# Strassen's seven block products for most of the down projection, in a one-core float32 decoder trunk

## The chip, the cores and the metric

The kernel runs on one core of a Trainium2 chip. The metric is the device time of one execution in microseconds (us), the median of three runs. The engines are named as the profile names them: PE (matmul) with PEld (its weight load), DVE (VectorE), ACT (ScalarE), POOL (GpSimd) and SP (SyncE, whose queue issues most loads).

## The reference, cut to what matters

One layer over 512 tokens of width 1024: a SwiGLU, a token mixer, a second SwiGLU, each added to the running `x`. The change touches the two SwiGLUs only.

```
D_MODEL, SEQ, D_FF, DEPTH = 1024, 512, 2816, 1
def swiglu(x, w_gate, w_up, w_down):
    return (jax.nn.silu(x @ w_gate) * (x @ w_up)) @ w_down
...
x = x + 0.5 * swiglu(rms_norm(x, ffn1_norm[i]), ffn1_w_gate[i], ffn1_w_up[i], ffn1_w_down[i])
x = x + token_mixer(rms_norm(x, mix_norm[i]), ...)
x = x + 0.5 * swiglu(rms_norm(x, ffn2_norm[i]), ffn2_w_gate[i], ffn2_w_up[i], ffn2_w_down[i])
```

## The kernel before, in words

Every float32 product in question is made of three matmuls: an operand is split into a high part of type float32r and a low part (the rest), and high times high, high times low and low times high are summed in PSUM (`mm3`, L443; the matmul itself is L448). A split of weights is one ACT copy (`whi`, L100) and one subtraction (`wlo`, L101); a split of activations is the same pair in `split` (L453, L454).

The hidden width 2816 is cut into 22 tiles of 128 columns, called ff tiles here. `ffn` (L505) goes through them in eleven rounds p, two ff tiles a round. A round makes the gate tiles g0 and g1 (24 matmuls of 512 tokens each), then the up tiles u0 and u1. After a gate tile ACT takes a tanh of it (`th`, L517) and DVE makes `m` (L519). After an up tile DVE makes the activation `a` (L524), and `a` is split into `ah` and `al`. Gate tiles go to the three PSUM banks of `mm`, up tiles and down products to the three of `sc`.

The down projection is laid between the gate and the up tiles. In rounds 2, 4, 6 and 8 `down` (L556) multiplies a chunk of four finished ff tiles by their rows of the down weights: 2 column halves x 4 token tiles x 4 ff tiles x 3 = 96 matmuls of 512 columns. Each of its eight PSUM tiles is added to the running `x` on DVE by one instruction (`add_x`, L541). Round 9 does ff tiles 16 and 17, and after the last round comes a tail with ff tiles 18 to 21, both through `down_tile` (L543).

`Weights` (L61) streams all weights in one fixed order. `load` (L77) issues a DMA of 1 MB on SP's queue into one of two raw buffers; `split` (L85) splits the next part; `get` (L107) asks for a part that is to be used now; `bg` (L114) splits one more part if it is at most two (by default) ahead of the one in use. The split parts lie in four buffers each of `whi` and `wlo`. In the SwiGLUs the subtraction is on DVE (`self.sub`). Each engine does its instructions in the order in which the program gives them, and a waiting instruction holds what is behind it.

The pool `big2` has six tiles of 128x2048, four of which hold the normalised input `hT` in a SwiGLU. The pool `big` has 19 tiles of 128x1024 (`t4`) for `x`, the split activations and much else. After round 0 the hook `hook0` (L634) issues six small loads on POOL's queue (`setup_loads`, L395), and after round 2 `hook2` (L637) does small work with them (`setup_work`, L413), two small matmuls on PE among it.

Of the kernel before, what the change touches and what calls it, by code (L numbers as in the profile page):

```python
# [11 lines left out]
F32 = mybir.dt.float32  # L12
# [48 lines left out]
class Weights:  # L61


    def __init__(self, nc, raw_pool, pool, specs, ahead_load):
        self.nc, self.raw_pool, self.pool, self.specs = nc, raw_pool, pool, specs
# [6 lines left out]
        self.order = [(s, p) for s, spec in enumerate(specs) for p in range(len(spec[1]))]  # L72
# [12 lines left out]
    def split(self, last):  # L85
        nc = self.nc
        while self.n_split <= min(last, len(self.order) - 1):
            i = self.n_split
            s, p = self.order[i]
            self.load(s)  # L90
            src = self.specs[s][1][p](self.raws[s])
            a, b = src.shape[1], src.shape[2]
            if (self.specs[s][2], p) in self.held:
# [7 lines left out]
            self.sub.tensor_tensor(l, src, h.bitcast(F32), op=ALU.subtract)  # L101
            self.parts[s, p] = (h, l)
            self.n_split += 1
            if p == len(self.specs[s][1]) - 1:
                self.load(s + self.ahead_load)

    def get(self, name, p):  # L107
        s = self.ids[name]
        i = self.first[s, p]
        self.split(i)  # L110
        self.cur = max(self.cur, i)
        return self.parts[s, p]
# [87 lines left out]
def hybrid_trunk_kernel(ctx: ExitStack, tc: tile.TileContext, x, rel_bias, ffn1_norm, ffn1_w_gate, ffn1_w_up,  # L200
# [42 lines left out]
    specs = []  # L243

    def cols(w, name, c0):

        def view(raw):
            return raw.rearrange("p (k c) -> p k c", k=8)
        specs.append(([(view, w[:, c0:c0 + 256].rearrange("(k p) c -> p k c", p=128))],
                      [lambda raw, g=g: view(raw)[:, :, g * 128:g * 128 + 128] for g in range(2)], name))  # L250

    def cols256(w, name, c0):
# [4 lines left out]
        specs.append((loads, parts, name))  # L257

    def rows(w, name, r0, nk, c0, nc_):
# [5 lines left out]
        specs.append((loads, parts, name))  # L265
# [19 lines left out]
    for i in range(2):  # L285
        src = w_in[512 * i:512 * i + 512]
        specs.append(([(lambda raw, o=o, n=n: c_view(raw)[:, :, o:o + n],
                        src[:, c:c + n].rearrange("(k p) c -> p k c", p=128))
                       for o, c, n in ((0, C_Q, 384), (384, IDX_K, 72))],
                      [lambda raw, h=h: c_view(raw)[:, 2 * h:2 * h + 2, :] for h in range(2)], f"c{i}"))  # L290
# [3 lines left out]
    def cols2x(name, c0, c1):  # L294
# [5 lines left out]
        specs.append((loads, [lambda raw, h=h: view(raw)[:, 4 * h:4 * h + 4, :] for h in range(2)], name))  # L300
# [9 lines left out]
    def row_cols(w, name):  # L310

        def view(raw):
            return raw.rearrange("p (k c) -> p k c", k=2)
        specs.append(([(view, w.rearrange("(k p) c -> p k c", p=128))],
                      [lambda raw, h=h: view(raw)[:, :, 512 * h:512 * h + 512] for h in range(2)], name))
# [21 lines left out]
    W = Weights(nc, rawp, wsp, specs, 2)  # L337
# [167 lines left out]
    def ffn(f, hT, order, hooks, after_tile):  # L505
# [25 lines left out]
        def down_terms(c, nk, t, wparts, csl):  # L531
            terms = []
            per = nk // 2
            for k in range(nk):
                w = wparts[k // per]
                ah, al = aT[4 * c + k]
                terms.append((ah[:, tok(t)], al[:, tok(t)], w[0][:, k % per, csl], w[1][:, k % per, csl]))
            return terms

        def add_x(ps, t, csl):  # L540
# [825 lines left out]
```

## Time and profile before

| | |
|---|---|
| median of three runs | 1312.66 us (1312.38 to 2589.32) |
| the profiled execution | 1312.75 us |
| its span, first to last instruction | 1310.8 us |
| mean granted TensorE clock | 0.997 of full speed |

The span is what the views of the trace cover. The profiled execution has 1.95 us outside of it. One of the three runs, 2589.32 us, is about twice as long as the other two and is left out of the comparison.

### The profile page before, as it was taken

To read this page: it belongs to the slowest core of one execution; us is meant where nothing else is said; L and a number is where in the kernel's file an instruction comes from. 1 tells how busy PE (TensorE), PEld (TensorE's weight loads), DVE (VectorE), ACT (ScalarE), POOL (GpSimd) and SP (SyncE) were. 2 spreads that over 40 slices of the span, in tenths; PEclk is the share of its full clock that TensorE was granted. 3 is DMA by queue.
4 is the path that set the end of the run, shared out by engine and by line. 5 is a ranking of instruction groups with operands and counts; after the bars stand their busy time and mean duration, and the time that the engine had idled before them with its cause. 6 is when DMAs were issued, how large, how long until landed. Compare 5 with 4: busy or idle time off the path is not lost.

```text
span 1310.8 us, 17140 instructions
## 1 busy us (share of the span) xinstructions
PE 1293.1 (99%) x6976; PEld 1097.5 (84%) x6976; DVE 677.9 (52%) x1265; ACT 451.7 (34%) x832; POOL 153.7 (12%) x137
## 2 busy tenths in 40 slices
PE   9999999999999999999989999999999999999998
PEld 8887888888889889889877778888898888888887
DVE  4444444445464666587854564447644444444453
ACT  4322222222343545454566432233332222222220
POOL 3000000000011435446340000000000000000000
PEclk9999999999999999999999999999999999999999
DMA  6233323222332222222222034423232323332321
GB/s 202 97 97 116 96 96 96 97 97 96 122 129 68 95 82 77 86 65 81 65 82 62 23 102 137 157 68 106 87 97 96 97 96 97 96 97 96 96 96 65
DMA packets 101777, 125.07 MB, mean 95 GB/s; under 512 B 3817, under 2 KB 85225, under 8 KB 101698
## 3 DMA queue, kind: packets, MB, share of 16 engines
q1 hardware_dynamic: 96690, 114.08, 27.1%
q10 hardware_dynamic: 3456, 5.24, 1.2%
q0 software_dynamic: 1552, 4.65, 1.2%
q8 instruction: 55, 0.90, 0.3%
q14 instruction: 24, 0.20, 0.0%
HBM read 119.13 MB, written 4.84 MB: 95 GB/s over the span
## 4 chain that ended last, share of the span: by engine, by line
PE 92%; DVE 3%; ACT 2%; DMA 1%; issue 0%; POOL 0%; ACTq 0%; DVEq 0%
PE u L448 18%; PE dn L448 18%; PE g L448 18%; PE gt L448 10%; PE wo L448 3%; PE br L448 3%; PE iq L448 2%; PE c L448 2%; PE b0q L448 1%; PE a0q L448 1%; PE a0v L448 1%; PE a0k L448 1%; PE a2q L448 1%; PE a1v L448 1%; PE b0v L448 1%; PE a1k L448 1%
## 5 line engine op out<-in xcount | busy, mean ns | idle before, releaser
L100 ACT ACTIVATE whi<-raw 128x1024 fp32r<-128x1024 f32 (+1 forms) x210 | 218.8, 1051 | 182.3 <-PE dn L448 141.2
L101 DVE TENSOR_TENSOR wlo<-raw,whi 128x1024 fp32r<-128x1024 f32 (+1 forms) x178 | 216.3, 1220 | 75.4 <-ACT whi L100 75.1
L448 PE MATMUL dn<-whi,ah 128*128 128x512 f32 x352 | 137.1, 389 | 0.0
L448 PE MATMUL dn<-whi,al 128*128 128x512 f32 x352 | 137.0, 389 | 0.0
L448 PE MATMUL dn<-wlo,ah 128*128 128x512 f32 x352 | 136.9, 389 | 0.0
L541 DVE SCALAR_TENSOR_TENSOR x<-dn,x 128x512 f32<-128x512 f32 x96 | 65.8, 690 | 108.3 <-PE dn L448 108.1
L453 ACT ACTIVATE ah<-a 128x512 fp32r<-128x512 f32 x44 | 27.8, 632 | 190.2 <-DVE a L524 190.2
L519 DVE SCALAR_TENSOR_TENSOR m<-th,g 128x512 f32<-128x512 f32 x44 | 30.2, 687 | 116.2 <-ACT th L517 116.2
L101 POOL TENSOR_TENSOR wlo<-raw,whi 128x1024 fp32r<-128x1024 f32 x32 | 76.7, 2397 | 28.6 <-ACT whi L100 18.6
L524 DVE TENSOR_TENSOR a<-m,u 128x512 f32<-128x512 f32 x44 | 30.2, 687 | 95.4 <-PE u L448 95.4
L448 PEld LDWEIGHTS dn<-whi,al 128*128 128x128 f32 x352 | 66.1, 188 | 13.8
L448 PEld LDWEIGHTS dn<-wlo,ah 128*128 128x128 f32 x352 | 66.1, 188 | 13.7
L448 PEld LDWEIGHTS dn<-whi,ah 128*128 128x128 f32 x352 | 66.1, 188 | 13.6
L448 PE MATMUL gt<-rmh,wlo 128*128 128x512 f32 x192 | 76.2, 397 | 0.0
L448 PE MATMUL gt<-rml,whi 128*128 128x512 f32 x192 | 76.0, 396 | 0.0
L448 PE MATMUL gt<-rmh,whi 128*128 128x512 f32 x192 | 76.0, 396 | 0.0
L517 ACT ACTIVATE th<-g 128x512 f32<-128x512 f32 x44 | 26.3, 597 | 139.3 <-PE g L448 139.3
L448 PE MATMUL g<-hal,whi 128*128 128x512 f32 (+1 forms) x192 | 71.4, 372 | 0.3 <-DVE hal L454 0.3
L448 PE MATMUL g<-hah,whi 128*128 128x512 f32 (+1 forms) x192 | 71.6, 373 | 0.1
L448 PE MATMUL g<-hah,wlo 128*128 128x512 f32 (+1 forms) x192 | 71.4, 372 | 0.2 <-POOL wlo L101 0.2
L448 PE MATMUL g<-hbh,whi 128*128 128x512 f32 (+1 forms) x192 | 71.4, 372 | 0.0
L448 PE MATMUL u<-hah,wlo 128*128 128x512 f32 (+1 forms) x192 | 71.4, 372 | 0.0
(1086 smaller groups left out, 3042.8 us busy)
## 6 DMA issues: line engine op xcount, KB each, us to landing
raw<-in_w_in SPq DMA_DIRECT2D x25, 1024.0 KB, 5.1
raw<-in_ffn_w_gate SPq DMA_DIRECT2D x22, 1024.0 KB, 5.2
raw<-in_ffn_w_up SPq DMA_DIRECT2D x22, 1024.0 KB, 5.1
raw<-in_ffn_w_down SPq DMA_DIRECT2D x22, 1024.0 KB, 4.9
raw<-in_w_in SPq DMA_DIRECT2D x8, 512.0 KB, 4.5
raw<-in_w_out SPq DMA_DIRECT2D x4, 1024.0 KB, 4.7
x<-in_x SPq DMA_DIRECT2D x4, 512.0 KB, 6.5
x1d<-x ACTq DMA_DIRECT2D x4, 512.0 KB, 2.7
```

Source lines behind the costliest of these rows:

```text
L100: nc.scalar.activation(h, src, AF.Copy)
L101: self.sub.tensor_tensor(l, src, h.bitcast(F32), op=ALU.subtract)
L448: nc.tensor.matmul(ps, l, r, start=i == 0 and q == 0, stop=i == n - 1 and q == 2)
L453: nc.scalar.activation(hi, src, AF.Copy)
L517: nc.scalar.activation(th, g, AF.Tanh, scale=0.5)
L519: nc.vector.scalar_tensor_tensor(m, th, 1.0, g, op0=ALU.add, op1=ALU.mult)
L524: nc.vector.tensor_tensor(a, m, u, op=ALU.mult)
L541: nc.vector.scalar_tensor_tensor(xt[t][:, csl], ps, 0.25, xt[t][:, csl], op0=ALU.mult, op1=ALU.add)
```

## The change

The first sixteen ff tiles (four chunks c of four) are multiplied by Strassen's scheme. For a pair of ff tiles the left operand is cut into four blocks: even or odd ff tile, first or second 256 tokens. The weights of a chunk are cut likewise: even or odd rows of 128, left or right half of the 1024 columns. Seven products replace eight. A product has two PSUM tiles of 128 tokens by 512 columns, and each of them takes 2 pairs x 3 = 6 matmuls of 512 columns, 12 for the product.

- **Left sums.** `left_blocks` makes five sums or differences of 128x256 for a pair of ff tiles on POOL. Splits of 128x256, 128x1024 and 128x512 for each pair follow on ACT and DVE, the last two of them (`split_sums`) only after the next gate or up tile has been issued.
- **Weight sums.** A new class `Blocks` loads a chunk's 2 MB as two tiles into the two free tiles of `big2` and makes five sums of 128x1024 for a chunk on POOL, most of them in place. The split of each of the seven weight blocks has its subtraction on POOL and no longer on DVE. The loads of the next chunk are issued on SP when the seventh block of this one is split, and have to wait until that split has been done.
- **Results.** Two products out of three go into two blocks of the output: a chunk has 24 additions to `x` in place of 8.
- **Order.** In rounds 2 to 9 one product (`down_block`) comes after each gate or up tile: four in an even round, three in an odd one. Their PSUM tiles alternate between `mm` and `sc`. The split order is written out as `plan`.
- **Moved.** Ff tiles 16 and 17 are multiplied in round 10 and not in round 9; `hook2` runs after round 1 and not after round 2.

```diff
+            name, p = self.order[i]
+            block = self.blocks.get(name)
+            sub = self.sub
+            if block is not None:
+                src, sub = block.part(p), nc.gpsimd
...
             nc.scalar.activation(h, src, AF.Copy)
-            self.sub.tensor_tensor(l, src, h.bitcast(F32), op=ALU.subtract)
+            sub.tensor_tensor(l, src, h.bitcast(F32), op=ALU.subtract)
...
+            if block is not None:
+                block.after(p)
+            elif p == len(self.specs[s][1]) - 1:
                 self.load(s + self.ahead_load)
...
+class Blocks:
+    def __init__(self, nc, new_tile, new_spare, srcs, then):
+        self.nc, self.new_tile, self.new_spare, self.srcs, self.then = nc, new_tile, new_spare, srcs, then
+
+    def load(self):
+        v = []
+        for h, src in enumerate(self.srcs):
+            tile_ = self.new_tile(h)
+            self.nc.sync.dma_start(tile_, src)
+            v.append((tile_[:, 0:4:2, :], tile_[:, 1:4:2, :]))
+        (self.b11, self.b21), (self.b12, self.b22) = v
+
+    def part(self, p):
+        if p == 0:
+            self.spare = self.new_spare()
+            self.sum(self.spare, self.b12, self.b22, ALU.subtract)
+        return (self.spare, self.b11, self.b22, self.spare, self.b12, self.b11, self.b21)[p]
+
+    def sum(self, out, a, b, op):
+        self.nc.gpsimd.tensor_tensor(out, a, b, op=op)
+
+    def after(self, p):
+        if p == 1:
+            self.sum(self.spare, self.b11, self.b22, ALU.add)
+        elif p == 2:
+            self.sum(self.b12, self.b11, self.b12, ALU.add)
+        elif p == 3:
+            self.sum(self.b11, self.b21, self.b11, ALU.subtract)
+        elif p == 4:
+            self.sum(self.b21, self.b21, self.b22, ALU.add)
+        elif p == 6:
+            self.then()
...
     def ffn_specs(f):
         wg, wu, wd = ffn_w[f]
+        for c in range(4):
+            src = wd[c * 512:c * 512 + 512].rearrange("(k p) c -> p k c", p=128)
+            blocks[f"w{f}{c}"] = Blocks(
+                nc, lambda h, c=c: big2.tile([128, 4, 512], F32, tag="hT", name=f"raww{f}{c}{h}"),
+                lambda c=c: t4(f"rawe{f}{c}").rearrange("p (k c) -> p k c", k=2),
+                [src[:, :, h * 512:h * 512 + 512] for h in range(2)],
+                lambda c=c: c < 3 and blocks[f"w{f}{c + 1}"].load())
         for p in range(11):
-            cols(wg, f"g{f}{p}", 256 * p)
-            c = p // 2 - 1
-            if p % 2 == 0 and 0 < p < 10:
-                rows(wd, f"d{f}{c}_0", c * 512, 4, 0, 512)
-                rows(wd, f"d{f}{c}_1", c * 512, 4, 512, 512)
-            if p == 9:
+            between = p in range(2, 10)
+            cols(wg, f"g{f}{p}", 256 * p, not between)
+            if p == 10:
                 rows(wd, f"d{f}4", 16 * 128, 2, 0, 1024)
-            cols(wu, f"u{f}{p}", 256 * p)
+            cols(wu, f"u{f}{p}", 256 * p, not between)
+            if between:
+                for i, (kind, j) in enumerate((("g", 0), ("g", 1), ("u", 0), ("u", 1))):
+                    plan.append((f"{kind}{f}{p}", j))
+                    if p % 2 * 4 + i < 7:
+                        plan.append((f"w{f}{p // 2 - 1}", p % 2 * 4 + i))
...
             nc.vector.tensor_tensor(a, m, u, op=ALU.mult)
+            if ff < 16:
+                left_blocks(ff, a)
+                return
...
+        def left_blocks(ff, a):
+            c, pr = ff // 4, ff // 2 % 2
+            plus = lambda out, l, r, op=ALU.add: nc.gpsimd.tensor_tensor(out, l, r, op=op)
+            if ff % 2 == 0:
+                if pr == 0:
+                    aT["a11", c] = t4(f"a11{f}{c}", F32R).rearrange("p (r x t) -> p r x t", r=2, x=2)
+                split(aT["a11", c][:, pr, 0, :], aT["a11", c][:, pr, 1, :], a[:, T1])
+                sums = t4(f"sum{f}{ff}").rearrange("p (s t) -> p s t", s=4)
+                firsts[0] = (a, sums)
+                plus(sums[:, 3, :], a[:, T2], a[:, T1], ALU.subtract)
+                return
+            a0, sums = firsts.pop(0)
+            plus(sums[:, 0, :], a0[:, T2], a[:, T2])
+            plus(sums[:, 1, :], a0[:, T1], a[:, T2])
+            plus(sums[:, 2, :], a[:, T1], a[:, T2], ALU.subtract)
+            plus(a[:, T1], a0[:, T1], a[:, T1])
+
+            def split_sums():
+                hl = aT["s", c, pr] = [t4(f"s{x}{f}{ff}", F32R).rearrange("p (s t) -> p s t", s=4) for x in "hl"]
+                split(hl[0], hl[1], sums)
+                aT["a_2", c, pr] = t4k(f"a_2{f}{ff}")
+                split(aT["a_2", c, pr][:, 0, :], aT["a_2", c, pr][:, 1, :], a)
+            late.append(split_sums)
...
+        INTO = ((0, 1, 1), (1, 1, 1)), ((1, 0, 1), (1, 1, -1)), ((0, 0, -1), (0, 1, 1)), ((0, 0, 1), (1, 1, 1)),             ((1, 1, 1),), ((0, 0, 1), (1, 0, 1)), ((0, 0, 1),)
+
+        def down_block(c, i):
+            w = W.get(f"w{f}{c}", i)
+            W.bg()
+            for u in range(2):
+                ps = (mm, sc)[u](f"dn{f}{c}{i}{u}")
+                drain(mm3(ps, [left(c, pr, i, u) + (w[0][:, pr, :], w[1][:, pr, :]) for pr in range(2)]))
+                for hr, hc, sign in INTO[i]:
+                    add_x(ps, 2 * hr + u, HALVES[hc], sign)
...
+            if p == 1:
+                blocks[f"w{f}0"].load()
...
-                    if p % 2 == 0 and 0 < p < 10:
-                        down(p // 2 - 1, 0)
-                        down(p // 2 - 1, 1)
-                    if p == 9:
+                    if p == 10:
...
                 mm_in(kind, p, j, ps[kind, j], s)
+                while late:
+                    late.pop()()
...
+                if p in range(2, 10):
+                    if p % 2 * 4 + step < 7:
+                        down_block(p // 2 - 1, p % 2 * 4 + step)
+                    step += 1
...
-    ffn(0, hT, order, {0: hook0, 2: hook2, 8: lambda: load_gain(1, mix_norm, nc.gpsimd)}, after1)
+    ffn(0, hT, order, {0: hook0, 1: hook2, 8: lambda: load_gain(1, mix_norm, nc.gpsimd)}, after1)
```

## Rows read from the trace of the kernel before

**Rows 1.** The page: busy us (share of span) xinstructions by engine; clock by slice.

```profile
PE 1293.1 (99%) x6976; PEld 1097.5 (84%) x6976; DVE 677.9 (52%) x1265; ACT 451.7 (34%) x832; POOL 153.7 (12%) x137
...
PEclk9999999999999999999999999999999999999999
```

**Rows 2.** Busy time in one stretch: PE, PEld, DVE, ACT, POOL, clock, DMA share, GB/s.

```profile
117.00:182.28 65.28, 65.28 (x290) 54.05 (x289) 28.05 (x32) 16.64 (x21) 0.00 (x0) 1.00 0.31 97
```

**Rows 3.** Timeline of DVE: start us, us, what, [idle before it, and its releaser].

```profile
41.91 0.68 DVE L524 TENSOR_TENSOR a<-m,u 128x512 f32<-128x512 f32 x1
...
61.00 0.69 DVE L524 TENSOR_TENSOR a<-m,u 128x512 f32<-128x512 f32 x1 [1.88 <-PE u L448]
...
99.08 0.69 DVE L524 TENSOR_TENSOR a<-m,u 128x512 f32<-128x512 f32 x1 [3.61 <-PE u L448]
104.52 0.69 DVE L524 TENSOR_TENSOR a<-m,u 128x512 f32<-128x512 f32 x1 [1.88 <-PE u L448]
...
152.18 0.69 DVE L541 SCALAR_TENSOR_TENSOR x<-dn,x 128x512 f32<-128x512 f32 x1 [0.90 <-PE dn L448]
154.90 0.69 DVE L541 SCALAR_TENSOR_TENSOR x<-dn,x 128x512 f32<-128x512 f32 x1 [2.03 <-PE dn L448]
```

**Rows 4.** Groups by line and shape: count, busy us, mean ns, idle before.

```profile
L100 ACT ACTIVATE whi<-raw 128x1024 fp32r<-128x1024 f32 x206 | 214.9, 1053 | 182.3 <-PE dn L448 141.2 <-PE g L448 16.7 <-PE gt L448 14.8
L101 DVE TENSOR_TENSOR wlo<-raw,whi 128x1024 fp32r<-128x1024 f32 x174 | 211.9, 1223 | 72.6 <-ACT whi L100 72.3
L448 PE MATMUL dn<-whi,ah 128*128 128x512 f32 x352 | 137.1, 389 | 0.0
...
L101 POOL TENSOR_TENSOR wlo<-raw,whi 128x1024 fp32r<-128x1024 f32 x32 | 76.7, 2397 | 28.6 <-ACT whi L100 18.6 <-DMA biasa<-tab 6.2 <-issue 3.9
...
L541 DVE SCALAR_TENSOR_TENSOR x<-dn,x 128x512 f32<-128x512 f32 x96 | 65.8, 690 | 108.3 <-PE dn L448 108.1
...
L454 DVE TENSOR_TENSOR al<-a,ah 128x512 fp32r<-128x512 f32 x44 | 30.5, 692 | 30.7 <-ACT ah L453 30.7
...
L453 ACT ACTIVATE ah<-a 128x512 fp32r<-128x512 f32 x44 | 27.8, 632 | 190.2 <-DVE a L524 190.2
```

**Rows 5.** Timeline of POOL: the shortest and the longest one-input copy.

```profile
406.16 0.29 POOL L956 COPY work<-cm 128x128 f32<-128x128 f32 x1
...
580.16 2.06 POOL L1260 CAST rml<-hml 128x1024 fp32r<-128x1024 f32 x1
```

**Rows 6.** Timeline of DVE from 436 us.

```profile
437.69 3.07 DVE L970 SCALAR_TENSOR_TENSOR work<-rl,cw,work 128x512 f32<-128x512 f32 x2 [1.80 <-ACT rl L969]
...
441.53 1.60 DVE L970 SCALAR_TENSOR_TENSOR work<-rl,cw,work 128x512 f32<-128x512 f32 x2
...
443.97 1.56 DVE L458 TENSOR_SCALAR a0qn2v<-a0qn2ss 128x4 f32<-128x4 f32 x1
...
448.53 0.17 DVE L458 TENSOR_SCALAR a0qn3v<-a0qn3ss 128x4 f32<-128x4 f32 x1
```

**Rows 7.** Timeline of POOL beside it.

```profile
436.96 2.40 POOL L101 TENSOR_TENSOR wlo<-raw,whi 128x1024 fp32r<-128x1024 f32 x1
...
443.12 2.38 POOL L101 TENSOR_TENSOR wlo<-raw,whi 128x1024 fp32r<-128x1024 f32 x1
```

**Rows 8.** Loads of the whole run: KB each, median us from issue to landing.

```profile
raw<-in_ffn_w_down SPq DMA_DIRECT2D x22, 1024.0 KB, 4.9
```

**Rows 9.** Loads issued in the first 12 us.

```profile
raw<-in_ffn_w_up SPq DMA_DIRECT2D x1, 1024.0 KB, 11.3
```

**Rows 10.** Stretch 6 to 8 us, columns as in rows 2.

```profile
6.00:8.00 2.00, 2.00 (x6) 1.22 (x6) 1.33 (x3) 1.15 (x2) 0.56 (x1) 1.00 1.05 369
```

**Rows 11.** Timeline of POOL: first and last issue of `hook0`.

```profile
18.45 1.55 POOL L399 DMA_DIRECT2D qkg<-in_qk_gain  x2
...
22.14 0.53 POOL L410 DMA_DIRECT2D tabm<-in_tabmask  x1
```

**Rows 12.** Landing of two of these loads, from the view of their tile.

```profile
DMA to landing us min/median/max: 4.0/4.2/4.4
```

More of the change, by code (lines that the diff above doesn't have):

```diff
@@ L71, in __init__ @@
         self.held, self.held_tile = (), None
-        self.order = [(s, p) for s, spec in enumerate(specs) for p in range(len(spec[1]))]
+        self.order = plan
         self.first = {sp: i for i, sp in enumerate(self.order)}
@@ L240, in stat, with add_spec, cols @@
         return small.tile([128, w], F32, tag=f"st{w}", name=name, bufs=12 if w == 4 else 8)[:, :n]
-    specs = []
-    def cols(w, name, c0):
+    specs, plan, blocks = [], [], {}
+    def add_spec(loads, parts, name, planned=True):
+        specs.append((loads, parts, name))
+        if planned:
+            plan.extend((name, p) for p in range(len(parts)))
+    def cols(w, name, c0, planned=True):
         def view(raw):
             return raw.rearrange("p (k c) -> p k c", k=8)
-        specs.append(([(view, w[:, c0:c0 + 256].rearrange("(k p) c -> p k c", p=128))],
-                      [lambda raw, g=g: view(raw)[:, :, g * 128:g * 128 + 128] for g in range(2)], name))
+        add_spec([(view, w[:, c0:c0 + 256].rearrange("(k p) c -> p k c", p=128))],
+                 [lambda raw, g=g: view(raw)[:, :, g * 128:g * 128 + 128] for g in range(2)], name, planned)
     def cols256(w, name, c0):
@@ L256, in cols256 @@
         parts = [lambda raw, h=h: raw.rearrange("p (k c) -> p k c", k=8)[:, 4 * h:4 * h + 4, :] for h in range(2)]
-        specs.append((loads, parts, name))
+        add_spec(loads, parts, name)
     def rows(w, name, r0, nk, c0, nc_):
@@ L299, in cols2x @@
                   w_in[:, c:c + 128].rearrange("(k p) c -> p k c", p=128)) for g, c in enumerate((c0, c1))]
-        specs.append((loads, [lambda raw, h=h: view(raw)[:, 4 * h:4 * h + 4, :] for h in range(2)], name))
+        add_spec(loads, [lambda raw, h=h: view(raw)[:, 4 * h:4 * h + 4, :] for h in range(2)], name)
     def a_specs(g):
@@ L313, in view @@
             return raw.rearrange("p (k c) -> p k c", k=2)
-        specs.append(([(view, w.rearrange("(k p) c -> p k c", p=128))],
-                      [lambda raw, h=h: view(raw)[:, :, 512 * h:512 * h + 512] for h in range(2)], name))
+        add_spec([(view, w.rearrange("(k p) c -> p k c", p=128))],
+                 [lambda raw, h=h: view(raw)[:, :, 512 * h:512 * h + 512] for h in range(2)], name)
     a_specs(0)
@@ L529, in act_u @@
             split(aT[ff][0], aT[ff][1], a)
[L531 to L540, printed above, removed]
-            nc.vector.scalar_tensor_tensor(xt[t][:, csl], ps, 0.25, xt[t][:, csl], op0=ALU.mult, op1=ALU.add)
+        T1, T2 = slice(0, 256), slice(256, 512)
@@ new lines, in ffn @@
+        firsts, late = {}, []
+        def left_blocks(ff, a):
[20 more added lines that the diff above has]
+            late.append(split_sums)
@@ new lines, in left @@
+        def left(c, pr, i, u):
+            cs = slice(128 * u, 128 * u + 128)
+            if i == 0:
+                return tuple(aT["a11", c][:, pr, x, cs] for x in range(2))
+            if i in (2, 5):
+                cs = slice(cs.start + 256, cs.stop + 256) if i == 5 else cs
+                return tuple(aT["a_2", c, pr][:, x, cs] for x in range(2))
+            return tuple(hl[:, {1: 0, 3: 1, 4: 3, 6: 2}[i], cs] for hl in aT["s", c, pr])
+        INTO = ((0, 1, 1), (1, 1, 1)), ((1, 0, 1), (1, 1, -1)), ((0, 0, -1), (0, 1, 1)), ((0, 0, 1), (1, 1, 1)),             ((1, 1, 1),), ((0, 0, 1), (1, 0, 1)), ((0, 0, 1),)
@@ L554, in down_tile @@
                 add_x(ps, t, csl)
-        def down(c, half):
-            parts = [W.get(f"d{f}{c}_{half}", p) for p in range(2)]
-            for t in range(NT):
-                if t % 2 == 0:
-                    W.bg()
-                ps = sc(f"dn{f}{c}{half}{t}")
-                drain(mm3(ps, down_terms(c, 4, t, parts, slice(0, 512))))
-                add_x(ps, t, slice(512 * half, 512 * half + 512))
         for p in range(11):
             ps, ms = {}, {}
-            W.cap = W.first[W.ids[f"u{f}0"], 1] if p == 0 else 1 << 30
+            step = 0
+            if p == 1:
+                blocks[f"w{f}0"].load()
+            W.cap = W.first[f"u{f}0", 1] if p == 0 else 1 << 30
             todo = order if p == 0 else [("g", 0, ALL), ("g", 1, ALL), None, ("u", 0, ALL), ("u", 1, ALL)]
@@ L625, in u_part @@
     def u_part(f, p):
-        return lambda: W.split(W.first[W.ids[f"u{f}0"], p])
+        return lambda: W.split(W.first[f"u{f}0", p])
     lo2, hi2 = slice(0, 256), slice(256, 512)
```

35 lines of the change are left out of this document (18 added, 17 removed).

## The prediction

> **What bounds the kernel now.** I read the page first: PE is busy for 1293.1 of 1310.8 us at a clock of nine tenths or more in every slice [rows 1]. Busy PE is not yet PE at its rate, so the next view is one stretch of the first SwiGLU. From 117.00 to 182.28 lie exactly two rounds, one of them with a chunk of the down projection: 192 gate and up matmuls and 96 down matmuls, 288 in all (the row counts 290, two being cut by the edges). PE is busy for all 65.28 us, so one matmul costs 65.28 / 288 = 0.2267 us; DVE works 28.05 us of them, ACT 16.64 and POOL nothing [rows 2]. The timeline of DVE says the same twice: up tiles of 24 matmuls end 5.44 us apart, down tiles of 12 end 2.72 us apart [rows 3]. A matmul's own duration in the groups, 389 ns [rows 4], overlaps with the next one's and is no cost. So in the SwiGLUs a matmul that goes away is worth 0.2267 us for as long as nothing else becomes late, and no wait is there to be gained.
>
> **The matmuls.** Down products take 3 x 352 = 1056 matmuls now [rows 4]. A chunk has 96, with the change 7 x 12 = 84. Two SwiGLUs have eight chunks: 8 x 12 = 96 matmuls fewer, 96 x 0.2267 = 21.76 us. The moving tile stays 512 columns wide, so I take the same price for those that remain. Two rounds should then take 65.28 - 2.72 = 62.56 us. Call this a period; all budgets below are for one.
>
> **DVE.** Away go four weight subtractions at 1.22 and four of `al` at 0.69 [rows 4]: 7.7 us. To come are 16 more additions to `x` at 0.69, 11.0, and for each of two pairs low parts of 1024, 512 and 256 columns: 1.22, 0.69 and, priced as if of 512, 0.69, together 5.2. 28.05 [rows 2] - 7.7 + 11.0 + 5.2 = 36.6 of 62.56 us. **ACT** loses 4 x 1.05 + 4 x 0.63 and gains 7 x 1.05 + 2 x (1.05 + 0.63 + 0.63) [rows 4]: 16.64 - 6.7 + 12.0 = 21.9 us. Neither is full, so their added work costs nothing while PE covers it. Without that cover the 11.0 us of additions alone would eat the 2.72 us four times over.
>
> **POOL** goes from nothing to seven weight subtractions and five weight sums of 1024 columns, two inputs each, at 2.40 [rows 4]: 28.8 us. The ten sums of 256 columns have no row. One-input copies took 0.29 us for 128 columns and 2.06 for 1024 [rows 5], so time goes with columns: a quarter of 2.40 is 0.6, and the upper bound is the whole 2.40. I take 0.75, near the lower end because of those two copies: 7.5 us, 36.3 in all (34.8 to 52.8).
>
> **DVE and POOL together.** They get in each other's way. Two DVE instructions with two inputs in SBUF took 3.07 us where the same pair took 1.60 later, and a tiny one took 1.56 in place of 0.17 [rows 6]; each time a POOL subtraction ran beside it, to 439.36 and to 445.50 [rows 7], and DVE came free 0.7 us (one instruction) after the one end and right at the other. The Trainium skill, page "SBUF — State Buffer", section "Who interferes with whom", calls this an exclusive lock: a DVE instruction with two SBUF inputs and a GpSimd instruction that reads SBUF block each other for a whole instruction. It speaks against this change, which puts weight work on POOL, and these rows agree with it. So what must fit into a period is the sum: POOL's 36.3, and of DVE the eight gate and up subtractions (9.8) and the 5.2 above, 51.3 of 62.56 us. The additions to `x` and `m` and `a` have one input in PSUM and I leave them out. By this sum nothing is lost; with POOL's upper bound it would be 67.8, and then the change loses (rival 2).
>
> **Waits added, walked through by hand.** A round is now steps of tile (5.44) and block (2.72), 8.16 us. A block's weights are split from the start of the block before it, 8.16 us ahead of their use: ACT 1.05 + POOL 2.40, and the sum for a later block 2.40 behind that. In an odd up step five POOL instructions more (3.0 to 3.8 us) go ahead of them: 7.3 us, still in time. DVE waits for at most one POOL instruction, 2.40, with two to four additions queued behind. Three PSUM banks in each pool are reused after 8 us or more. `split_sums` may hold ACT's queue, and the tanh behind it, until POOL has its sums, some 3 us; the tanh's bank is wanted again 8 us later. In my walk none of these reaches PE.
>
> The narrowest place is **the change of chunk**. Let the last gate tile of a chunk end at 0: the seventh weight block is split from there (tanh 0.6, ACT 1.05, POOL 2.40, with hand-offs 4.2 us). Only then does SP issue the next 2 MB, with the following up weights queued behind it. One MB takes 4.9 us to land [rows 8]; a second adds 1.05 MB / 369 GB/s = 2.8 [rows 10]: 7.7 us, at most the 11.3 of a load that stood behind two others [rows 9]. Landed at 11.9 (15.5). Sum 2.40, ACT 1.05, subtraction 2.40, hand-offs 0.3: ready at 18.1 (21.7). The first block is wanted after block, up tile, block, up tile and gate tile: 2.72 + 5.44 + 2.72 + 5.44 + 5.44 = 21.8. The margin is 3.7 us (0.1), less what the lock adds. It occurs three times a SwiGLU; the first chunk is loaded in round 1, with some 20 us to spare.
>
> **Moved steps.** `hook0` now stands behind the left sums of round 0, whose last activation is made at 41.91 [rows 3]. So its loads go at about 45.6 and not at 18.45; six issues take 4.2 us [rows 11], landing at most 4.4 [rows 12]: 54.3. `hook2` now wants them at the end of round 1, at 61.0 [rows 3]. PE covers that with 6.7 us to spare; if not, PE stands for the difference, once. The load of ff tiles 16 and 17 comes a round later with the same lead. Nothing in the mixer changes.
>
> **Sum.** 1312.75 (profiled; median 1312.66, 0.09 less) - 21.76 = 1291.0; half a us for first blocks that are a little late: **1291.5 us**, 1.6% less.
>
> **Rivals.**
> 1. *The chunk change stalls PE.* If the lock or slower loads take more than the 3.7 us, each further us costs PE six. Loads as in rows 9 use up all but 0.1 of the margin, and one or two POOL instructions of 2.40 in the way of the chain do the rest: 2 to 3 us six times, 12 to 18 us, 1303 to 1309. For it: three hand-overs in series through POOL. Against: SP has a free way to the memory then, and loads at a third of DMA time [rows 2].
> 2. *POOL and the shared port become the bound*, the slower side. If a 256-column sum costs as much as a 1024-column one, a period needs 67.8 us and not 62.56: eight times 5.2 is 42, 1333 us. It begins to decide where the sum passes 62.56 (short sums of 1.9 us) and makes the kernel slower than before past 65.28 (2.15 us). Against: the copies [rows 5] grow with columns. For: POOL's short instructions in the trace are one-input ones only. Under this rival the lock of the section above is what makes POOL's time and DVE's add; if the two could overlap, POOL's 52.8 would fit.
> 3. *A matmul costs more beside the added POOL and DVE work*, or the clock falls. Three per cent on the 2112 + 960 matmuls of the SwiGLUs (696 us) is 21 us and eats the gain. Against: the clock stays up in all slices [rows 1], the mixer's with their POOL work among them. About 1300 to 1312.
> 4. *The change saves less than it says.* If `down_block` had 14 matmuls a product, nothing would be saved: 1312.7. The loop counts 2 tiles x 2 pairs x 3 = 12, so I give this next to nothing.
>
> **How the numbers follow.** Forecast, 1290 to 1294: 0.74. Rival 1, with any stall between 3 and 20 us: 0.13. Rival 2, at its bound or past it with a wait that my walk missed: 0.07. Rival 3: 0.04. Rival 4: none. Still below 1290, from gaps that I overlooked: 0.02. The range 1289 to 1302 holds the forecast and the milder half of rival 1, with the unknown costs of the walk (11 us for 1.8 us at each chunk change) inside: 0.82. Two per cent, 26 us, is about what a measurement of this kernel can tell from no change; PE has only 21.8 us to give, so faster by over 2% has 0.02. Slower by over 2% needs 1339, just past the upper bound of rival 2, so I give it half of that rival's and a little more: 0.04. Within: 0.94.
>
> **What would show it.** Right: 960 down matmuls, PE at 0.2267 us each without idle in rounds 2 to 9, a period of 62.6 us, DVE near 37, POOL near 36 in it, longer DVE subtractions beside POOL. Rival 1: an idle PE before the first block of a chunk, released by POOL's subtraction. Rival 2: POOL without gaps, PE waiting at most blocks. What would make me wrong most easily is the chain at the chunk change and a short POOL sum that is not short.

## The result, and the profile after

The changed kernel takes 1290.58 us, the median of four runs (1289.7 to 1292.1), against 1312.38 for the kernel before beside it (three runs); the ratio of the means is 0.9838 [0.9819, 0.9857]. The forecast was 1291.5. (A fourth run of the kernel before, 2589.32 us, is left out here, while the median of 1312.66 in the table ahead still has it in it.) The change is smaller than two per cent and all the same clear of the noise of about 0.2 per cent, so the prediction's limit of 26 us for what can be told from no change was too wide. The profiled execution took 1292.1 us, its span 1290.0.

The page of the kernel after (busy us, share and instructions by engine; clock by slice) answers to [rows 1]:

```profile
PE 1273.0 (99%) x6880; PEld 1081.7 (84%) x6880; DVE 798.7 (62%) x1377; ACT 484.1 (38%) x872; POOL 475.8 (37%) x313
...
PEclk9999999999999999999989999999999999999999
```

PE has 96 matmuls fewer and is still busy for 99%. One slice, in the mixer, fell to eight tenths. Two rounds of the first SwiGLU, columns as in [rows 2], from one `a` of an odd round to the same one two rounds later:

```profile
116.47:179.02 62.55, 62.55 (x277) 51.81 (x276) 44.77 (x46) 20.84 (x25) 40.43 (x22) 1.00 0.30 101
```

A period was 65.28 us [rows 2] and is 62.55, with PE busy throughout. DVE went from 28.05 to 44.77 us of it, ACT from 16.64 to 20.84, POOL from nothing to 40.43. The groups by line and shape (count, busy us, mean ns, idle before), which answer to [rows 4], say why DVE and POOL are above what was forecast (`raww` and `rawe` are tiles of `Blocks`):

```profile
L107 DVE TENSOR_TENSOR wlo<-raw,whi 128x1024 fp32r<-128x1024 f32 x142 | 215.2, 1522 | 58.5 <-ACT whi L106 58.2
...
L644 DVE SCALAR_TENSOR_TENSOR x<-dn,x 128x512 f32<-128x512 f32 x224 | 143.4, 682 | 30.0 <-PE dn L507 27.5
...
L150 POOL TENSOR_TENSOR raww<-raww,raww 128x1024 f32<-128x1024 f32 x16 | 54.3, 3396 | 0.0
...
L513 DVE TENSOR_TENSOR sl<-sum,sh 128x1024 fp32r<-128x1024 f32 x16 | 32.8, 2047 | 28.5 <-ACT sh L512 28.5
...
L600 POOL TENSOR_TENSOR sum<-a 128x256 f32<-128x256 f32 x32 | 23.5, 736 | 98.6 <-DVE a L583 77.0 <-PE u L507 21.6
```

The weight subtraction on DVE has a mean of 1522 ns where it had 1223, one of the same size on the left sums 2047, while the additions to `x`, with an input in PSUM, kept their 0.68. On POOL the 24 weight sums made in place take 3.4 us and not 2.40, the 16 into the tile `spare` 2.55 in the mean. Of the short sums 48 take 0.74, as assumed; the 32 right behind `a` take 0.94 in the mean. Two timelines of the kernel after show the mechanism (start us, us, what). DVE:

```profile
95.91 3.23 DVE L107 TENSOR_TENSOR wlo<-raw,whi 128x1024 fp32r<-128x1024 f32 x1
99.06 3.42 DVE L513 TENSOR_TENSOR sl<-sum,sh 128x1024 fp32r<-128x1024 f32 x1
```

and POOL beside it:

```profile
95.65 2.40 POOL L107 TENSOR_TENSOR wlo<-raww,whi 128x1024 fp32r<-128x1024 f32 x1
98.00 3.40 POOL L150 TENSOR_TENSOR raww<-raww,raww 128x1024 f32<-128x1024 f32 x1
```

The reader is to put the four ends in order: POOL 98.05, DVE 99.14, POOL 101.40, DVE 102.48. The steps between them are 1.09, 2.26 and 1.08 us, about one undisturbed instruction each (1.22, 2.40, 1.22). So the engines take turns here, and each record contains the wait for the other engine's turn. This is what the Trainium skill, page "SBUF — State Buffer", section "Who interferes with whom", calls an exclusive lock; here it works in both directions.

**Where the 21.8 us came from.** In the trace the last addition to `x` of the first SwiGLU began at 379.8 us before and begins at 368.6 after: 11.2 us. The view of these additions (durations in ns, first and last start in us), before and after:

```profile
L541 DVE SCALAR_TENSOR_TENSOR x<-dn,x x16: 679/684/692, 315.4 to 379.8; 128x512 f32<-128x512 f32 x16
L644 DVE SCALAR_TENSOR_TENSOR x<-dn,x x18: 679/684/692, 307.6 to 368.6; 128x512 f32<-128x512 f32 x18
```

From the first `m` of the second SwiGLU to its last addition to `x` it is 343.85 us before and 333.00 after, 10.85 less. DVE's timeline before:

```profile
963.12 0.68 DVE L519 SCALAR_TENSOR_TENSOR m<-th,g 128x512 f32<-128x512 f32 x1
...
1306.97 0.69 DVE L541 SCALAR_TENSOR_TENSOR x<-dn,x 128x512 f32<-128x512 f32 x1 [2.03 <-PE dn L448]
```

and after:

```profile
953.17 0.68 DVE L578 SCALAR_TENSOR_TENSOR m<-th,g 128x512 f32<-128x512 f32 x1
...
1286.17 0.69 DVE L644 SCALAR_TENSOR_TENSOR x<-dn,x 128x512 f32<-128x512 f32 x1 [2.03 <-PE dn L507]
```

The mixer between them, which the change does not touch, took 1.3 us of it back in these two executions: in one stretch of it the clock was 0.83 in the kernel after (columns as in [rows 2]), where no stretch of 20 us was below 0.91 before.

```profile
660.00:680.00 20.00, 16.84 (x114) 14.82 (x114) 8.06 (x44) 13.80 (x48) 6.02 (x4) 0.83 0.27 74
```

So the span shows 20.8 us, though the two SwiGLUs gave 22.05 (forecast 21.76); the medians differ by 21.8. The granted clock also goes with the spread of single runs: the kernel before took 1310.6 to 1310.8 us where its mean was 1.000 and 1312.5 to 1313.0 where it was 0.997. Differences of a microsecond or two between whole runs therefore say little, while in the periods shown here the clock is 1.00.

### The profile page after: what moved, and what is told of

Read it like the earlier page. It is cut to its first block, busy times and chain, and to the rows that moved or that the text cites. A ratio compares the mean times of both kernels' runs of the same rounds, so it can differ in the third digit from the quotient of the medians.

```text
span 1290.0 us, 17385 instructions
## 1 busy us (share of the span) xinstructions
PE 1273.0 (99%) x6880; PEld 1081.7 (84%) x6880; DVE 798.7 (62%) x1377; ACT 484.1 (38%) x872; POOL 475.8 (37%) x313
## 5 line engine op out<-in xcount | busy, mean ns | idle before, releaser
L106 ACT ACTIVATE whi<-raw 128x1024 fp32r<-128x1024 f32 (+1 forms) x178 | 185.5, 1050 | 64.8 <-PE u L507 26.5
L644 DVE SCALAR_TENSOR_TENSOR x<-dn,x 128x512 f32<-128x512 f32 x224 | 143.4, 682 | 30.0 <-PE dn L507 27.5
L107 POOL TENSOR_TENSOR wlo<-raww,whi 128x1024 fp32r<-128x1024 f32 x40 | 99.5, 2487 | 96.6 <-ACT whi L106 96.6
L507 PE MATMUL u<-hbh,wlo 128*128 128x512 f32 (+1 forms) x192 | 71.4, 372 | 0.0
L507 PE MATMUL u<-hah,whi 128*128 128x512 f32 (+1 forms) x192 | 71.4, 372 | 0.0
L507 PE MATMUL u<-hbh,whi 128*128 128x512 f32 (+1 forms) x192 | 71.4, 372 | 0.0
L507 PE MATMUL g<-hbl,whi 128*128 128x512 f32 (+1 forms) x192 | 71.3, 372 | 0.0
L507 PE MATMUL g<-hbh,wlo 128*128 128x512 f32 (+1 forms) x192 | 71.3, 371 | 0.0
L507 PE MATMUL u<-hbl,whi 128*128 128x512 f32 (+1 forms) x192 | 71.3, 371 | 0.0
L507 PE MATMUL u<-hal,whi 128*128 128x512 f32 (+1 forms) x192 | 71.3, 371 | 0.0
```

The lines of the kernel that those rows point to most:

```text
L106: nc.scalar.activation(h, src, AF.Copy)
L507: nc.tensor.matmul(ps, l, r, start=i == 0 and q == 0, stop=i == n - 1 and q == 2)
L644: nc.vector.scalar_tensor_tensor(xt[t][:, csl], ps, 0.25 * sign, xt[t][:, csl], op0=ALU.mult, op1=ALU.add)
```

## The experiments

The theory: PE is the bound, 96 matmuls fewer are the whole gain, and all added work lies beside PE, with reserves that can be read from the trace. The rivals: the added work eats part of a larger gain; POOL and DVE together are close to being the bound; the chunk change has next to no reserve.

### The saving alone, without the added work

The kernel before, with one of the eight PSUM tiles of each chunk left out (so the output lacks these products):

```diff
+                if half == 1 and t == 3:
+                    continue
                 ps = sc(f"dn{f}{c}{half}{t}")
```

> The kernel before, with one of a chunk's eight down tiles (last token tile, right half: 12 matmuls and one addition to x) left out in rounds 2, 4, 6 and 8, so that the output lacks it. Theory (only the matmul count matters, the added work of the change is hidden): the same saving as the change, 96 x 0.2267 = 21.8 us, 1290.7 us, ratio 0.983. Rival (the change pays something for its sums, splits and additions, and would otherwise save more): below 1289, beyond the change by what it pays.

Measured: 1291.2 us (1290.81 to 1291.63), ratio 0.984 [0.9825, 0.9855]. DVE's timeline shows the same period without any of the new work on POOL:

```profile
119.57 0.69 DVE L524 TENSOR_TENSOR a<-m,u 128x512 f32<-128x512 f32 x1 [2.63 <-PE u L448]
...
182.13 0.69 DVE L524 TENSOR_TENSOR a<-m,u 128x512 f32<-128x512 f32 x1 [2.64 <-PE u L448]
```

62.56 us. Leaving the products out brings what Strassen's scheme brings; the added sums, splits and additions cost nothing that these intervals, of about 2 us to either side, could show, and nothing in the period.

### The added work alone, without the saving

The kernel after, with the seventh product of each chunk multiplied twice; only one column of the repetition is copied out, into a tile that nobody reads:

```diff
+            eighth = stat(f"e{f}{c}{i}", 1)
...
+            if i == 6:
+                for u in range(2):
+                    ps = (mm, sc)[u](f"dx{f}{c}{i}{u}")
+                    drain(mm3(ps, [left(c, pr, i, u) + (w[0][:, pr, :], w[1][:, pr, :]) for pr in range(2)]))
+                    nc.vector.tensor_copy(eighth, ps[:, :1])
```

> The changed kernel with an eighth product a chunk: the seventh is multiplied once more into PSUM and not added. Theory: the 96 matmuls come back and nothing else, 1290.6 + 21.8 = 1312.4 us, ratio 1.000. Rival (part of the gain comes from something else, such as the order of the steps or the moved hook): the ratio stays under 0.995.

Measured: 1312.63 us (1310.97 to 1314.36, ten runs), ratio 1.0006 [0.9997, 1.0016]. DVE's timeline, at the copy from the repetition:

```profile
122.52 0.40 DVE L647 COPY e<-dx 128x1 f32<-128x1 f32 x2
...
187.80 0.40 DVE L647 COPY e<-dx 128x1 f32<-128x1 f32 x2
```

65.28 us, the period of [rows 2] to the hundredth. Together the two runs split the change: in a period the matmuls are all of the gain, and the rest is nothing.

### The weight work on DVE

```diff
-                src, sub = block.part(p), nc.gpsimd
+                src = block.part(p)
...
-        self.nc.gpsimd.tensor_tensor(out, a, b, op=op)
+        self.nc.vector.tensor_tensor(out, a, b, op=op)
```

> The changed kernel with all weight sums and weight subtractions of the blocks on DVE, none on POOL. DVE goes from 44.8 busy us in a period of 62.56 to about 28.05 - 7.7 + 11.0 + 5.2 + 12 x 1.22 = 51.2, POOL from 40.4 to 7.3. Theory (neither engine bounds, the lock only stretches hidden work): PE stays without idle, 1290.6 us within 2; the remaining DVE subtractions fall from 1.5 to near 1.22 us. Rival (DVE's queue becomes late in order, additions to x behind weight work): PE idles some us a period, over 1300.

Measured: 1290.48 us (1290.07 to 1292.08), ratio 0.9833 [0.9817, 0.985], the same as the change. The same two rounds of this kernel, one step of the rounds further on (columns as in [rows 2]):

```profile
147.15:209.71 62.56, 62.56 (x277) 51.80 (x276) 48.41 (x58) 20.84 (x26) 10.02 (x11) 1.00 0.32 101
```

and its subtraction among the groups:

```profile
L107 DVE TENSOR_TENSOR wlo<-raw,whi 128x1024 fp32r<-128x1024 f32 x142 | 172.3, 1219 | 58.4 <-ACT whi L106 58.1
```

With twelve instructions more, DVE is busy for only 3.6 us more, since its own instructions are back at 1219 ns (51.2 us were expected and 48.41 measured; POOL, with the short sums alone, took 10.02 for the expected 7.3). Where the weight work stands makes no difference to the time as long as PE covers it. The Trainium skill, page "GPSIMD Engine Reference", section "3.1 Elementwise — side-by-side cycle accounting", has GpSimd at about half of VectorE's speed for such an addition; the durations agree (2.40 against 1.22 us), and yet the choice is worth nothing here.

### How much more POOL holds

POOL gets additions of 128x1024 that write a scratch tile which nobody reads, after the splits of three of the seven blocks, or of all:

```diff
+            self.spare, self.scratch = self.new_spare(), self.new_spare()
...
+        if p in (0, 2, 5):
+            src = self.b21 if p > 4 else self.b22
+            self.sum(self.scratch, src, src, ALU.add)
```

(`range(7)` in the second kernel.) With three:

> The changed kernel with three more POOL sums of 1024 columns a chunk, to a tile that nobody reads, behind the splits of the blocks 0, 2 and 5: 7.2 us a period. By the sum of POOL and two-input DVE work a period needs 51.3 + 7.2 = 58.5 of 62.56 us. Theory: not bound, 1290.6 us, up to 3 more where a block's margin is only 2 to 4 us. Rival (POOL is bound by its chain of waits, not by its sum): over 1300.

Measured: 1291.38 us in one run (the kernel before beside it, on the same chip: 1310.79 in one run); no loss. With seven:

> Seven such sums a chunk, one behind each block's split: 16.8 us a period, 51.3 + 16.8 = 68.1. Theory (the two engines' SBUF work excludes each other, so that their sum is the bound): 68.1 - 62.56 = 5.5 us a period, eight times, 1335 us. Rival (only POOL's own time counts, 36.3 + 16.8 = 53.1 of 62.56): no stall beyond some us at blocks with small margins, 1291 to 1300.

Measured: 1307.05 us in one run, between the two expectations. A period of this kernel, and then its waits of PE (what for, us in total, times, longest):

```profile
127.74:193.30 65.56, 63.16 (x278) 51.67 (x276) 43.19 (x46) 20.93 (x26) 57.38 (x30) 1.00 0.30 96
```

```profile
PE dn L510 <- POOL wlo L107: 13.0, 12, 1.8
```

So neither the theory's 1335 nor the rival's 1291 to 1300 came. A period is 3.0 us longer and PE stands for 2.4 of them. Adding the row means gave the 51.3 us of the prediction, but consecutive records overlap a little. I laid the records of POOL and of DVE's instructions with two SBUF inputs over each other in one period of the timelines and took the time covered by either: 48.1 us with the change, 53.4 with three additions more, 60.7 of 65.56 with seven. The sum was some 3 us too high. What matters more: PE began to wait while 4.9 us of a period were still free. The waits sit at two blocks, the fifth (1.4 to 1.8 us) and the sixth (0.6), in this period at 168.0 and 177.07. Where the free time lies explains it:

```profile
138.13:181.23 43.10, 40.70 (x178) 33.07 (x177) 33.18 (x37) 14.14 (x17) 43.02 (x21) 1.00 0.24 74
```

From the second block's split to the seventh's POOL has no gap but one of 0.08 us, and both waits lie in this stretch; nearly all of the 4.9 us lie at the change of chunk, where POOL stood 2.5 to 2.8 us for the next load. So POOL, with DVE's turns in its records, is full there, although a mean over the period says that it is not.

### The reserve at the chunk change

POOL makes the first sum of a later chunk three times, or five times, in place of once:

```diff
-            self.sum(self.spare, self.b12, self.b22, ALU.subtract)
+            for _ in range(1 + 2 * self.later):
+                self.sum(self.spare, self.b12, self.b22, ALU.subtract)
...
+            blocks[f"w{f}{c}"].later = c > 0
```

(`4 * self.later` in the second.) First the undisturbed chain in the kernel after, POOL's timeline:

```profile
109.93 2.40 POOL L107 TENSOR_TENSOR wlo<-raww,whi 128x1024 fp32r<-128x1024 f32 x1 [5.19 <-ACT whi L106]
117.23 0.74 POOL L600 TENSOR_TENSOR sum<-a 128x256 f32<-128x256 f32 x1 [4.90 <-DVE a L583]
117.92 2.60 POOL L150 TENSOR_TENSOR rawe<-raww 128x1024 f32<-128x1024 f32 x1
121.69 2.40 POOL L107 TENSOR_TENSOR wlo<-rawe,whi 128x1024 fp32r<-128x1024 f32 x1 [1.17 <-ACT whi L106]
```

and PE's, where the two blocks are wanted:

```profile
99.94 0.39 PE L507 MATMUL dn<-whi,sh 128*128 128x512 f32 x1
...
129.86 0.39 PE L507 MATMUL dn<-whi,a 128*128 128x512 f32 x1
```

The seventh split ends at 112.33 and the first of the next chunk at 124.09; PE wants it at 129.86, so the reserve is 5.8 us (6.0 to the first matmul with the low part), where 3.7 were forecast. Three sums:

> The changed kernel; the first weight sum of the second to fourth chunk of each SwiGLU is done three times in place of once, so 4.8 us of POOL work more ahead of the chunk's first split. The trace of the changed kernel shows that split ready 5.8 us before its use. Theory (the margin is a real reserve): PE does not idle in the SwiGLUs, 1290.6 us within 2. Rival (other waits hang on this place, such as the left splits on ACT behind it): some us at each of six places, 1300 or more.

Measured: 1298.26 us in one run. Both extra sums together took 5.8 us, and the first block was just in time, as my number said; but the time rose by 7 us (6.9 above the run with three additions on the same chip, 7.7 above the median of the change) and the theory fell. POOL's timeline of this kernel, then one line of ACT's, then three of PE's:

```profile
117.72 8.40 POOL L151 TENSOR_TENSOR rawe<-raww 128x1024 f32<-128x1024 f32 x3
127.29 2.40 POOL L107 TENSOR_TENSOR wlo<-rawe,whi 128x1024 fp32r<-128x1024 f32 x1 [1.17 <-ACT whi L106]
```

```profile
132.80 1.06 ACT L514 ACTIVATE sh<-sum 128x1024 fp32r<-128x1024 f32 x1 [4.63 <-POOL sum L602]
```

```profile
137.84 0.39 PE L509 MATMUL dn<-whi,sh 128*128 128x512 f32 x1
138.35 0.50 PE L509 MATMUL dn<-wlo,sh 128*128 128x512 f32 x1
...
141.80 0.50 PE L509 MATMUL u<-hah,wlo 128*128 128x512 f32 x1 [0.20 <-DVE wlo L107]
```

POOL's left sums stand behind the delay, ACT's split of them (`sh`) waits 4.63 us for POOL, and the next weight splits stand behind that on ACT. So the second block and the following up tile come late: the block took 3.14 us and not 2.72, the tile 5.94 and not 5.44, together 0.9; at six chunk changes that is 5.5 of the 7 us. The prediction had named ACT's queue behind `split_sums` and put its hold at some 3 us. Five sums:

> The same sum five times, 9.6 us more POOL work. Theory: each of the six chunk changes stalls PE for 9.6 - 5.8 = 3.8 us and a little for the lock, 23 us in all, 1313 us; the wait is shown at the first block, released by POOL's subtraction. Rival (the chain has more slack than the trace shows, loads or ACT being what came last): under 1300.

Measured: 1332.21 us in one run, 41.6 more than the change. PE's waits:

```profile
PE dn L509 <- ACT whi L106: 14.8, 6, 3.0
...
PE dn L509 <- POOL wlo L107: 11.5, 6, 1.9
```

The four extra sums took 10.7 us here. The waits are 26.3 us, or 4.4 at each of the six chunk changes, near the 4.9 by which these sums exceed the reserve; the expected 3.8 had the sums at 2.40. The first part of each wait is for ACT's copy, which itself stood behind POOL's sums. The other 15 us come after the waits, at a lower clock. Stretches of 2 us at the first of them, columns as in [rows 2]:

```profile
130.00:132.00 2.00, 0.00 (x0) 0.00 (x0) 0.00 (x0) 0.93 (x1) 1.03 (x1) 1.00 0.00 0
132.00:134.00 2.00, 0.50 (x1) 0.19 (x1) 0.83 (x1) 1.07 (x2) 1.80 (x1) 0.68 0.00 0
134.00:136.00 2.00, 1.39 (x3) 1.16 (x4) 1.64 (x1) 0.00 (x0) 2.00 (x2) 0.50 0.00 0
136.00:138.00 2.00, 2.00 (x6) 1.55 (x5) 0.00 (x0) 0.37 (x1) 1.92 (x4) 0.50 0.39 109
138.00:140.00 2.00, 2.00 (x7) 1.52 (x7) 1.27 (x2) 2.00 (x4) 0.41 (x1) 0.61 1.06 376
```

The granted clock falls to 0.50, the 1.2 GHz level, while PE stands, and remains there for some 7 us, in which matmuls follow each other after 0.43 us and not 0.2267. From its first matmul to the next tile the block took 7.29 us where 2.72 are usual. At four of the six places the clock was low for 6.8 us, at the other two for 3.4, where the block took 6.61 and 6.65. All in all 41.6 / 6 = 6.9 us for a wait of 4.4.

### The reserve in the odd up step

The prediction's other thin place: the short sums that go ahead of a weight split in an odd round. Four more of them, 0.74 each:

```diff
-            plus(sums[:, 0, :], a0[:, T2], a[:, T2])
+            for _ in range(5 if pr == 0 and c else 1):
+                plus(sums[:, 0, :], a0[:, T2], a[:, T2])
```

> The changed kernel; the first of the four short POOL sums behind the second up tile of rounds 2, 4 and 6 is done five times in place of once: 4 x 0.70 = 2.8 us more POOL work ahead of the fifth block's split, six places in all. In the trace of the changed kernel this split is ready at 98.05 for a use at 99.94 + 0.23. Theory (the place with the least reserve is the fifth block, 2.1 us, and not the change of chunk, which bore 4.8 us without a wait at its first block): PE waits 0.7 us or a little more at each of the six, 4 to 6 us in all, 1295 to 1297. Rival (the reserve is as large as at the chunk change): no wait, 1290.6 us.

Measured: 1304.48 us in one run, 14 us more than the change (13 more than the change on the same chip) and well over the 1295 to 1297 that I expected. PE's waits:

```profile
PE dn L507 <- POOL wlo L107: 11.7, 6, 2.0
```

POOL's timeline and PE's:

```profile
92.64 5.65 POOL L600 TENSOR_TENSOR sum<-a,a 128x256 f32<-128x256 f32 x6 [0.91 <-DVE a L583]
...
99.77 2.36 POOL L107 TENSOR_TENSOR wlo<-raww,whi 128x1024 fp32r<-128x1024 f32 x1
```

```profile
99.83 0.39 PE L507 MATMUL dn<-whi,sh 128*128 128x512 f32 x1
102.18 0.63 PE L507 MATMUL dn<-wlo,sh 128*128 128x512 f32 x1 [1.96 <-POOL wlo L107]
```

With the change the fifth block's split ended at 98.05 for a use of its low part at 100.17 (the line of 99.94 above and one matmul): 2.1 us of reserve, or 1.9 if it is counted to the first matmul, as at the chunk change. Here it ended at 102.13. Six short sums took 5.65 us, 0.94 each, so they too took turns with DVE; the split came 4.1 us later for 3.0 us of added work, and PE stood 1.95 us, six times. The clock went down behind the first of the six waits alone. The 2 us after it, and the 2 us after the second (which ended at 168.56), columns as in [rows 2]:

```profile
102.00:104.00 2.00, 1.82 (x5) 1.42 (x6) 2.00 (x2) 0.97 (x2) 2.00 (x2) 0.60 0.00 0
168.00:170.00 2.00, 1.44 (x6) 1.22 (x7) 2.00 (x2) 1.36 (x2) 2.00 (x2) 1.00 0.01 2
```

Where it fell the block lasted 6.55 us, at the other five places 4.96 to 4.98, for a usual 2.72: 15 us in all, of which the waits are 11.7. The fifth block is the place with the least reserve, not the chunk change. In the trace of the change this holds for all 56 blocks: the fifth block of the first three chunks of each SwiGLU has 1.9 us to its first matmul, the other blocks have 2.6 to 4.5, and the change of chunk has the most, 5.3 to 5.8.

### One more chunk by Strassen's scheme

Ff tiles 16 to 19 as a fifth chunk: four products in round 10, three after the last round, and only ff tiles 20 and 21 in the old way.

```diff
-        for c in range(4):
+        for c in range(5):
...
-            between = p in range(2, 10)
+            between = p in range(2, 11)
...
-            if ff < 16:
+            if ff < 20:
...
+        for i in range(4, 7):
+            down_block(4, i)
```

> The changed kernel with a fifth chunk, ff tiles 16 to 19 in round 10, its last three products behind the last up tile; the tail keeps ff tiles 20 and 21. Theory (a product saved is 2.72 us wherever PE does not wait): 2 x 2.72 = 5.4 us less, 1285.2 us, ratio 0.979. Rival (the shorter tail, 2.72 us a token tile in place of 5.44, no longer covers the normalisation after it, or three products in a row outrun POOL): no gain, 1289 to 1295.

Measured: 1295.73 us (1295.11 to 1296.21), ratio 0.9874 [0.9859, 0.9889]: 5 us slower than the change, with 24 matmuls fewer. The end of the first SwiGLU, and PE's waits:

```profile
334.00:380.00 46.00, 39.02 (x173) 30.90 (x172) 36.09 (x52) 18.40 (x26) 16.88 (x10) 0.96 0.28 97
```

```profile
PE nt L541 <- DVE h L532: 5.4, 3, 1.9
...
PE dn L505 <- POOL wlo L107: 1.9, 2, 0.9
```

Only 39.02 of 46.00 us are PE's, where it was busy for all of them with the change. In the tail the next norm runs between the down products of the token tiles. DVE's instructions for a token tile are the same in both kernels, but the down products of a token tile now last 2.72 us and not 5.44, as the rival had it, and PE waits 1.7 to 1.9 us for `h` at three tiles; ahead of that DVE has the additions of three products in a row, and POOL's split comes 0.95 us late once in each SwiGLU. What each of these costs was not separated. So I kept the fifth chunk for the second SwiGLU alone and laid its seven products one, two, two and two between the tiles of round 10:

```diff
-        for c in range(4):
+        for c in range(4 + f):
...
+        if p == 10:
+            return ((0,), (1, 2), (3, 4), (5, 6))[i]
```

> The changed kernel with a fifth chunk (ff tiles 16 to 19) in the second SwiGLU alone, where no normalisation follows, its seven products spread over round 10: one, two, two, two behind the four tiles. Theory (the loss of the fifth chunk lies in the normalisation behind the first SwiGLU and in three products in a row): 2.72 us less than the changed kernel, 1287.9 us. Rival (two products a step outrun POOL, or the end of the kernel waits for DVE): no better than the changed kernel, 1290 to 1293.

Beside it, on the same chip, the change once more:

> The changed kernel once more, on the same chip as the next one: 1290.6 us, ratio 0.983 to 0.985.

Measured: 1290.19 us (1289.45 to 1290.74), ratio 0.9829 [0.9816, 0.9843], against 1291.7 (1290.48 to 1292.48), ratio 0.9839 [0.9826, 0.9853]. The intervals overlap, so it is not settled that this version is faster; it also changes two things at once, the place of the chunk and the spread of its products. In the two profiled executions the second SwiGLU alone, from its first `m` to its last addition to `x`, can be read from DVE's timeline; here for the fifth chunk:

```profile
952.39 0.68 DVE L583 SCALAR_TENSOR_TENSOR m<-th,g 128x512 f32<-128x512 f32 x1
...
1283.82 0.69 DVE L649 SCALAR_TENSOR_TENSOR x<-dn,x 128x512 f32<-128x512 f32 x1 [0.67 <-PE dn L512]
```

331.43 us, against 332.97 (953.46 to 1286.43) for the change: 1.5 of the 2.72 us that 12 matmuls are worth.

## Why the prediction was right, and where it was not

**The matmuls.** The term 96 x 0.2267 = 21.76 us was right as mechanism and as size: 1291.2 without the eighth tile, 1312.63 with it back, and periods of 62.56 and 65.28 us in the traces. The remaining matmuls kept their price. The half us on top, for first blocks that are late, had no such event behind it; that 1291.5 lies so near 1290.58 owes a little to luck.

**DVE, ACT, POOL.** ACT came to 20.8 us of a period for the forecast 21.9. DVE's 36.6 was 44.8 and POOL's 36.3 was 40.4. The counts were right, and an undisturbed short sum took 0.74 for the assumed 0.75 (rival 2's remark that POOL's short instructions have one input overlooks the 128x4 ones of L460, which have two, a power, and take 1.0 us or more); what I left out of the single engines' terms was the waiting for each other, though I had just read it from [rows 6]. POOL's sums at 3.4 us contain such waits and have no price of their own: with seven additions more on POOL the sum in place behind the fourth block's split, which has a mean of 3.38 with the change, took 2.38 to 2.42 us all eight times. It cost nothing, because PE covers 62.56 us.

**DVE and POOL together.** The sum of 51.3 us is 48.1 in the trace; its conclusion, that it fits, was right. Its rule was not: by it POOL holds 11 us more in any part of a period, and PE began to wait with seven additions while 4.9 were free, because these lay at the change of chunk and the stretch before the waits was full. The reading of [rows 6] behind it was loose in two places: the pair of 3.07 us ended 1.40 us after POOL, two instructions and not one, and the tiny instruction has one input in SBUF, so it is no case of the rule as the prediction words it. The records of 95 to 103 us above are the better evidence.

**The change of chunk.** "The narrowest place" is the step that failed, without effect on the time. Its margin was 5.8 us and not 3.7, for a reason that my walk, and the description of the change, had wrong. SP's timeline of the kernel after:

```profile
101.42 11.30 SPq L139 DMA_DIRECT2D raww<-in_ffn_w_down  x2
```

The first of the two loads goes at 101.42, before the seventh split: it waits for the fifth block's sum, which ends at 101.40 and is the last to read the tile. Only the second one waits for the split, to 112.33. So one MB and not two lies between that split and the next chunk's first sum, and the first split is ready 16.0 us after the last gate tile and not 18.1. The narrowest place is the fifth block with 2.1 us. My walk had the number for it, 7.3 of 8.16 us and so 0.9, but I priced only the step, called it in time and carried the smaller reserve no further. The first chunk, too, had no "some 20 us to spare": its loads go at 41.88 and 42.51, behind an up load, and the second lands at 53.90 for a use at 67.3. Its sum then stands on POOL behind a short sum that waits for DVE's `a` until 55.98, and the first split is done at 62.78, 4.5 us ahead of its use.

**Moved steps.** `hook0`'s loads go from 45.00 to 48.69, forecast 45.6 and on. The two small matmuls of `hook2` run at 60.5 without a wait of PE.

**The rivals.** None came about. Rival 1 needed more than 5.8 us at the chunk change, and even less does harm there, through ACT's queue; rival 2 needed more than three instructions of some 2.40 more on POOL in a period (no loss with three, 16 us with seven), and then showed part of its sign, POOL without gaps in one stretch of a period and PE waiting at two blocks of seven; rival 3's dearer matmul is excluded by the two periods; rival 4 by the count of 960 down matmuls. In the profiled pair the mixer lost 1.3 us. Its extra stretch at the lower clock began at 663.6 us, behind a wait of PE for ACT of 2.08 us (1.15 at the same place before); why that wait grew, and whether it alone lowered the clock, is not settled.

## What to carry to other kernels

Where one engine is busy without gaps, a change is worth the instructions that it takes from that engine, and work added to the others is free as long as each hand-over has a reserve. The reserve is a matter of single places: compare, block by block, when the last operand is ready and when it is wanted, and follow what stands behind a waiting instruction on every queue. Read how full an engine is in the stretch ahead of such a place and not over a whole period: PE began to wait where POOL had been without a gap for 30 us, while the period as a whole still had 4.9 us free. Where such cover ends, as in the tail, the same change can cost more than it saves.

## What the runs showed that was not expected

A wait of PE can cost more than its length, and not always the same: 4.4 us of it in one place cost 6.9 in the mean, because the clock then stood at 0.50 for 6.8 us in four places and 3.4 in two, and matmuls came 0.43 us apart; but of six waits of 1.95 us only one was followed by a lower clock, and of those of 1.4 to 1.8 us with seven additions on POOL none. A delay on POOL passes through ACT's queue to DVE and PE: 5.8 us that used up the direct reserve exactly still cost 0.9 us at each chunk change. And records of POOL and DVE contain each other's turns: a DVE subtraction of 1.22 us is recorded with as much as 3.42, a POOL sum of 2.40 with 3.40, so that busy shares of these two say less than the time that either of them covers.
